# A row gradient on one core: the first store of every three tiles waits for the second tile's vector pass, and Pool places the first tiles' row ends

## The chip, the cores and the metric

The kernel runs on one core of a Trainium2 chip. The metric is the device time of one execution in microseconds (us); before the change it is 1247.63 us, the median of three runs (1247.45 to 1247.71). The core has a vector engine (DVE), a general engine (POOL), a scalar engine (ACT) and a matrix engine (PE), of which the last two do nothing here, and a sync engine (SP), which issues all transfers. The transfers run on 16 DMA engines.

## The reference

`x` is an 8192 x 8192 array of float32, and the result is its gradient along the rows:

```python
def reference(x):
    return np.gradient(x, axis=1)
```

For an inner column `j` that is `(x[:, j+1] - x[:, j-1]) / 2`; for the first column it is `x[:, 1] - x[:, 0]`, for the last one `x[:, -1] - x[:, -2]`.

## The kernel before

The rows are cut into 32 tiles ("sets"). A tile holds 256 rows: each of the 128 partitions has `R` = 2 whole rows side by side, 2 x 8192 floats or 64 KB, so that a tile is 8.39 MB and one load or one store moves it in one piece. Three buffers, `slots[0]` to `slots[2]`, take the tiles in turn (`NB` = 3, tile `i` in slot `i % 3`). A slot is `SH` = 64 floats longer than a tile: a load fills it from position 64 on, and the result is written from position 0 on, so that the result overwrites the input in place, a little behind the reading.

For each tile the following is done, in the order of the program:

1. The load (line 60), issued by SP.
2. POOL's subtraction (line 70) computes the four row-end differences of each partition (two rows, two ends) and keeps them in the small buffer `ends`. It waits for the load.
3. DVE's pass (line 76) computes half the difference of the neighbours over the whole slot, 16382 elements per partition, in one instruction. It waits for step 2. The values at the row ends come out wrong there, since the pass runs over the seam between the two rows.
4. The placement (line 87) copies the four values from `ends` over the row ends. It waits for step 3 and runs on POOL for the tiles with `i % 5` equal to 1 or 3 (except for the last two tiles), else on DVE.
5. The store (line 89), issued by SP when the placement is done.

The order of the work is written out by hand (`manual_schedule`), and what waits for what is given by the helper `chain`, which keeps only the waits named in its arguments. SP works through its list in order, and so an instruction that waits holds up those behind it. The list is: loads 0, 1, 2; stores 0, 1, 2; loads 3, 4, 5; stores 3, 4, 5; and so on, with the loads of the next group of three behind the third store of the group before (line 91). Load `i` waits until store `i - 3` has landed, because it fills the same slot. The last group has two tiles only, 30 and 31.

Of the kernel before, what the change touches and what calls it, by code (L numbers as in the profile page):

```python
# [1 line left out]

# [4 lines left out]


@with_exitstack
def kernel(  # L10
    ctx: ExitStack,
    tc: tile.TileContext,
    x: bass.AP,
    out: bass.AP,
):

    nc = tc.nc
    P = nc.NUM_PARTITIONS
    n, m = x.shape
    R = 2
    NB = 3  # L30
    SH = 64
    W = R * m
    nsets = n // (P * R)
    f32 = x.dtype

    x_sets = x.rearrange("(s p t) m -> s p (t m)", p=P, t=R)
    out_sets = out.rearrange("(s p t) m -> s p (t m)", p=P, t=R)

    pool = ctx.enter_context(tc.tile_pool(name="pool", bufs=1))
    slots = [pool.tile([P, SH + W], f32, name=f"slot{k}", tag=f"slot{k}") for k in range(NB)]  # L40
    ends = pool.tile([P, nsets, R, 2], f32, name="ends", tag="ends")
    loads, stores = [], [None] * nsets
    in_front = {}

    def chain(i, ins, *needed):

        group, engine = f"slot{i % NB}", ins.ins.engine
        keep = [o.ins for o in needed]  # L50
        if in_front.get(engine, (None,))[0] == group:
            keep.append(in_front[engine][1])
        tc.declare_no_dep(ins.ins, group=group, keep=keep, reason="implied by the needed step")
        tc.add_to_no_dep_group(group, ins.ins)
        in_front[engine] = group, ins.ins
        return ins

    def load(i):
        b = slots[i % NB]
        ins = nc.sync.dma_start(out=b[:, SH : SH + W], in_=x_sets[i])  # L60
        loads.append(chain(i, ins, *([stores[i - NB]] if i >= NB else [])))

    with tc.manual_schedule():
        for i in range(NB):
            load(i)
        for i in range(nsets):
            b = slots[i % NB]
            xin = b[:, SH : SH + W].rearrange("p (t m) -> p t m", m=m)

            ins = nc.gpsimd.tensor_sub(  # L70
                out=ends[:, i, :, :],
                in0=xin[:, :, 1 : m : m - 2],
                in1=xin[:, :, 0 : m - 1 : m - 2],
            )
            at = [chain(i, ins, loads[i])]
            ins = nc.vector._custom_dve(  # L76
                dve_ops.TENSOR_TENSOR_REDUCE_SUB_MAX,
                out=b[:, 1 : W - 1],
                in0=b[:, SH + 2 : SH + W],
                in1=b[:, SH : SH + W - 2],  # L80
                s0=0.0,
                s1=0.5,
            )
            halved = chain(i, ins, *at)
            res = b[:, 0:W].rearrange("p (t m) -> p t m", m=m)
            placer = nc.gpsimd if i % 5 in (1, 3) and i < nsets - 2 else nc.vector
            ins = placer.tensor_copy(out=res[:, :, 0 : m : m - 1], in_=ends[:, i, :, :])  # L87
            placed = chain(i, ins, halved)
            ins = nc.sync.dma_start(out=out_sets[i], in_=b[:, 0:W])
            stores[i] = chain(i, ins, placed)  # L90
            if i % NB == NB - 1:
                for k in range(i + 1, min(i + 1 + NB, nsets)):
                    load(k)


# [1 line left out]
_INS = ['x']  # L97
_OUTS = [((8192, 8192), 'float32')]


# [23 lines left out]
```

## Time and profile before

| | |
|---|---|
| Median of three runs | 1247.63 us |
| The profiled execution | 1247.59 us, of which the span from the first to the last instruction is 1245.7 us |
| DVE's pass (line 76) | 32 times, 17224 ns each, 551.2 us in all |
| POOL's row-end differences (line 70) | 32 times, 198 ns each |
| Placements (line 87) | DVE 20 times, 172 ns each; POOL 12 times, 190 ns each |
| Moved by the DMA engines | 536.88 MB, half read and half written, 431 GB/s over the span |
| From issue to landing | load 58.0 us, store 40.4 us (medians); the shortest store 20.9 us |

The times of a row in the timeline are its start and its duration, counted from the start of the span; an "x1" is one instruction, and in brackets stands how long the engine had been idle before it, and what ended that. "SPq" is the issuing of transfers by SP; such a row tells when the transfer was handed over, not how long it took. From issue to landing a transfer also waits behind those that are queued before it.

### The profile page before, as it was taken

The numbers are of one execution on the slowest core, as the hardware profiler recorded it, in microseconds if no ns is written. First come the engines' busy times: TensorE is split into PE (matmuls) and PEld (weight loads), VectorE is DVE, ScalarE is ACT, GpSimd is POOL, SyncE is SP. The second block draws the span as 40 slices with busy tenths as digits, with TensorE's granted clock in tenths as the row PEclk, the third lists the DMA queues.
The fourth block names the chain that finished last, engine by engine and source line by source line (L and its number), as shares of the span: only waits on it lengthen the run. The fifth ranks groups of instructions, "written<-read, shape, count | busy, mean of one in ns | idle before, by whom it ended". The sixth has DMA issues, their size and how long they took to land.

```text
span 1245.7 us, 237 instructions
## 1 busy us (share of the span) xinstructions
DVE 554.6 (45%) x52; POOL 8.8 (1%) x48
## 2 busy tenths in 40 slices
DVE  2850583069009702850582079009603840591083
POOL 0000000000000000000000000000000000000000
DMA  9999999999999999999999999999999999999999
GB/s 404 438 436 423 427 431 438 438 438 436 436 427 431 425 438 436 425 434 436 429 434 436 434 436 434 436 434 438 419 436 436 434 438 438 431 434 429 429 410 404
DMA packets 9217, 536.88 MB, mean 431 GB/s; under 512 B 1024, under 2 KB 1024, under 8 KB 1024
## 3 DMA queue, kind: packets, MB, share of 16 engines
q1 hardware_dynamic: 9216, 536.88, 99.8%
q14 instruction: 1, 0.01, 0.0%
HBM read 268.44 MB, written 268.44 MB: 431 GB/s over the span
## 4 chain that ended last, share of the span: by engine, by line
another core or an unknown queue 74%; DVE 18%; DMA 3%; issue 2%; POOL 1%; SPq 0%; POOLq 0%
DVE slot L76 18%; DMA slot<-in_x_dram 3%; POOL ends L70 0%; POOL slot L87 0%; SPq L60 0%; POOLq L119 0%; DVE slot L87 0%
## 5 line engine op out<-in xcount | busy, mean ns | idle before, releaser
L76 DVE CUSTOM_DVE_ANT_0 slot<-slot 128x16382 f32<-128x16382 f32 x32 | 551.2, 17224 | 668.7 <-POOL ends L70 668.7
L70 POOL TENSOR_TENSOR ends<-slot 128x4 f32<-128x4 f32 x32 | 6.3, 198 | 989.6 <-DMA slot<-in_x_dram 989.6
L87 POOL COPY slot<-ends 128x4 f32<-128x4 f32 x12 | 2.3, 190 | 207.9 <-DVE slot L76 207.9
L87 DVE COPY slot<-ends 128x4 f32<-128x4 f32 x20 | 3.4, 172 | 0.7
L108 POOL MEMSET const-bfloat16-1.0<- 128x1 bf16 x1 | 0.1, 101 | 0.0
L108 POOL MEMSET const-uint8-127<- 128x1 uint8 x1 | 0.1, 101 | 0.0
L108 POOL MEMSET const-float32-0.0<- 128x1 f32 x1 | 0.1, 98 | 0.2 <-issue 0.2
L108 POOL MEMSET const-float32-1.0<- 128x1 f32 x1 | 0.1, 98 | 0.0
## 6 DMA issues: line engine op xcount, KB each, us to landing
slot<-in_x_dram SPq DMA_DIRECT2D x32, 58.0
out_dram<-slot SPq DMA_DIRECT2D x32, 40.4
```

The source lines that it names most:

```text
L70: ins = nc.gpsimd.tensor_sub(out=ends[:, i, :, :], in0=xin[:, :, 1 : m : m - 2], in1=xin[:, :, 0 : m - 1 : m - 2],)
L76: ins = nc.vector._custom_dve(dve_ops.TENSOR_TENSOR_REDUCE_SUB_MAX, out=b[:, 1 : W - 1], in0=b[:, SH + 2 : SH + W], in1=b[:, SH : SH + W - 2],
L87: ins = placer.tensor_copy(out=res[:, :, 0 : m : m - 1], in_=ends[:, i, :, :])
L108: nc = _bacc.Bacc("TRN2", target_bir_lowering=False, num_devices=1)
```

## The change

The placement of the first tile of each group of three (`i % NB == 0`) goes to POOL, and all the other ones to DVE. The store of such a first tile is moved in the program behind the second tile's pass, and gets a wait for that pass besides the one for its own placement. The last group of two tiles is left as it was: its stores wait only for their own placements, which are on DVE. The order of SP's list is the same as before.

```diff
+    def store(i, placed):
+        ins = nc.sync.dma_start(out=out_sets[i], in_=slots[i % NB][:, 0:W])
+        stores[i] = chain(i, ins, placed)
+        return ins
+
+    def store_behind(i, placed, other):
+        tc.add_manual_dep(
+            store(i, placed).ins,
+            other.ins.name,
+            mybir.DependencyInfo(mybir.DependencyClass.Sync, mybir.DependencyReason.DATA),
+            reason="the first store of a group goes behind the second tile's difference",
+        )
+
...
+            opens = i % NB == 1 and i < nsets - 2
...
-            halved = chain(i, ins, *at)
+            halved = chain(i, ins, halved)
+            if opens:
+                store_behind(i - 1, placed, halved)
             res = b[:, 0:W].rearrange("p (t m) -> p t m", m=m)
-            placer = nc.gpsimd if i % 5 in (1, 3) and i < nsets - 2 else nc.vector
+            placer = nc.gpsimd if i % NB == 0 and i < nsets - 2 else nc.vector
             ins = placer.tensor_copy(out=res[:, :, 0 : m : m - 1], in_=ends[:, i, :, :])
             placed = chain(i, ins, halved)
-            ins = nc.sync.dma_start(out=out_sets[i], in_=b[:, 0:W])
-            stores[i] = chain(i, ins, placed)
+            if i % NB or i >= nsets - 2:
+                store(i, placed)
```

More of the change, by code (lines that the diff above doesn't have):

```diff
@@ L4 @@
 import concourse.tile as tile
-from concourse import bass_utils, dve_ops
+from concourse import bass_utils, dve_ops, mybir
 from concourse._compat import with_exitstack
@@ L74 @@
             )
-            at = [chain(i, ins, loads[i])]
+            halved = chain(i, ins, loads[i])
             ins = nc.vector._custom_dve(
```

## The prediction

> **What bounds the kernel now.** I read the page's busy shares and DMA lines first, then the queues, the chain, and the timeline around one change from loads to stores.
>
> ```profile
> DVE 554.6 (45%) x52; POOL 8.8 (1%) x48
> DMA  9999999999999999999999999999999999999999
> ...
> q1 hardware_dynamic: 9216, 536.88, 99.8%
> ```
>
> No compute engine is half busy, while the 16 DMA engines are taken 99.8% of the span, all by one queue, the one SP issues. So the bound is 64 transfers of 8.39 MB (32 loads, 32 stores) one behind the other. A wait on DVE or POOL costs only if it lets this queue run dry. The chain of waits agrees: it gives 74% to "another core or an unknown queue" (its name here for transfers still in flight) and 18% to DVE's pass, which merely lies beside them.
>
> Next, the timeline from the end of tile 3's vector pass to that of tile 5 (second group of three; SPq rows are the issues; POOL L70 starts 0.07 us after a load has landed):
>
> ```profile
> 157.41 0.19 POOL L87 COPY slot<-ends 128x4 f32<-128x4 f32 x1 [17.32 <-DVE slot L76]
> 157.63 0.34 SPq L89 DMA_DIRECT2D out_dram<-slot  x1
> 159.25 0.20 POOL L70 TENSOR_TENSOR ends<-slot 128x4 f32<-128x4 f32 x1 [1.65 <-DMA slot<-in_x_dram]
> 159.48 17.22 DVE L76 CUSTOM_DVE_ANT_0 slot<-slot 128x16382 f32<-128x16382 f32 x1 [2.13 <-POOL ends L70]
> 176.74 0.17 DVE L87 COPY slot<-ends 128x4 f32<-128x4 f32 x1
> 176.94 0.34 SPq L89 DMA_DIRECT2D out_dram<-slot  x1
> 178.70 0.20 POOL L70 TENSOR_TENSOR ends<-slot 128x4 f32<-128x4 f32 x1 [19.25 <-DMA slot<-in_x_dram]
> ```
>
> Store 3 is issued at 157.63, a whole transfer before load 5 lands (178.63), so it waits in the queue behind loads 4 and 5. The next lines are the one place where a store is issued late, store 30 near the end (nothing is loaded behind load 31):
>
> ```profile
> 1186.93 0.20 POOL L70 TENSOR_TENSOR ends<-slot 128x4 f32<-128x4 f32 x1 [77.07 <-DMA slot<-in_x_dram]
> ...
> 1204.62 0.34 SPq L89 DMA_DIRECT2D out_dram<-slot  x1
> 1206.28 0.20 POOL L70 TENSOR_TENSOR ends<-slot 128x4 f32<-128x4 f32 x1 [19.14 <-DMA slot<-in_x_dram]
> ```
>
> Load 31 follows load 30 by 1206.28 - 1186.93 = 19.35 us. That is the undisturbed price of a transfer: eight packets of 64 KB on each DMA engine, 2.418 us each in the DMA records.
>
> **Where the queue loses time today.** Measure each group's third load the same way, by POOL L70's start for the third tile minus that for the second: 20.40 (42.04 to 62.44), 19.45, 19.51, 20.05, 19.85, 19.79, 19.45, 19.84, 19.33, 19.36. Minus 19.35 each, the excess is 1.05 + 0.10 + 0.16 + 0.70 + 0.50 + 0.44 + 0.10 + 0.49 - 0.02 + 0.01 = 3.53 us. The whole stretch from load 1 landed to load 31 landed (42.04 to 1206.28, 60 transfers) is 1164.24 - 60 x 19.35 = 3.24 us too long, so practically all the loss sits in these third loads. The DMA records place it: the last 64 KB packet of the third load, just before a store already queued, takes 2.5 to 3.8 us instead of 2.42, on most engines. At load 31, with no store queued until the last moment, the last packet is not stretched on any engine (excess at most 0.008 us).
>
> **The change, part by part.**
>
> *The late store.* Ten first stores (tiles 0, 3, ..., 27) now wait for the pass over the next tile. For tile 3: the pass over tile 4 ends at 159.48 + 17.22 = 176.70; SP follows a finished engine by 0.03 to 0.06 us in the rows above, so the issue goes from 157.63 to about 176.76, 19.1 us later. Behind it on SP's queue stand stores 4 and 5 and loads 6 to 8. Store 4 must follow the 0.34 us issue: about 177.1 instead of 176.94, not due at the engines until store 3 is through (about 197.9); the rest is issued from 196.39 on. So of the queue's items only store 3 itself can come late.
>
> *Does it come late?* Unstretched, load 5 lands at 159.18 + 19.35 = 178.53, 1.77 us after the new issue. Store 30 was issued 1206.21 - 1204.62 = 1.59 us before load 31 landed, and landed 20.9 us after its issue, at 1225.5: 19.3 us behind load 31, so nothing was lost. The changed stores have 0.18 us more. In the DMA records store 30's first packets start 0.84 to 1.22 us after the issue, which for store 3 is 177.60 to 177.98; the slowest engine is at work on load 5 until about 158.80 + 19.34 = 178.14. That engine sees no gap, by 0.16 to 0.54 us; faster ones do, but the landing waits for the slowest anyway. Bounds of this cost: 0 from store 30; above, the other transfer that started on an idle queue, load 0, landed 21.9 us after its issue, which would make store 3 land at 198.66 instead of 178.53 + 19.35 = 197.88, 0.78 us per group or 7.8 in ten. I take 0, because store 30 is the same kind of transfer in the same place, and load 0 is a cold start (its own first packets took 3 us).
>
> [...]
>
> *The stretched packet.* If the stretch comes from the store queued behind the load, as load 31 suggests, the late store removes it: 3.53 us at most. Bounds: the whole 3.53, or 0 if it is a property of the change from reading to writing; I take the whole, by the row of load 31, though loads 26 and 29 (-0.02 and 0.01) also show none with a store queued, so this row is weak evidence.
>
> *Re-alignment.* Today the 16 engines drift apart: the landings of one transfer spread over 0.6 us at the start, 3.0 at the end. A new store holds back engines more than the above margin ahead of the slowest, so each group starts nearly level, and small stretches on changing engines (first packets of a group's first load: up to 0.15, 0.34, 0.15, 0, 0.23, 0.13, 0.26, 0, 0.27, 0.20 us on the worst engine in the DMA records, 1.73 in all) can each become the slowest's. Bounds 0 and 1.73; I take half, 0.85, since the margin absorbs those on engines that are ahead.
>
> *Placements.* First tiles go to POOL (10 copies of 190 ns by L87's row), all second and third ones to DVE (172 ns). They lie in DVE's and POOL's idle time: after the copy at 157.41, POOL still waited 1.65 us for the next load, DVE 2.13. The store that follows is not due for 19 us. Cost 0; were that cover gone, 10 x 0.19 = 1.9 us. Nothing on DVE, POOL or SP waits newly but the stores.
>
> **Sum.** The profiled execution took 1247.59 us (span 1245.7, 1.9 around it), 0.04 below the median of the runs. 1247.59 - 3.53 + 0.85 + 0 = 1244.9.
>
> **The rivals.**
>
> *The stretch stays* (22%). It belongs to the turn from reads to writes, and the late store changes nothing. For: loads 26 and 29 were not stretched although a store was queued, so the queue alone does not decide. Then each group pays its worst engine: the records' maxima are 1.40, 0.40, 0.31, 0.78, 0.91, 0.53, 0.40, 0.71, 0.07, 0.35, sum 5.86 against 3.53 paid now, at most +2.3; or the same as now if margins absorb that. 1247.6 to 1249.9, mostly 1248.
>
> *Level engines make it worse* (15%, slower). The largest stretch, 1.05, came at the first group, when the engines stood within 0.6 us; at 3 us apart it was about 0. If the stretch grows when all turn at once, re-alignment gives every group the first one's price: 10 x 1.05 - 3.53 = +7.0, 1254.6. It decides from a mean of 0.60 us per group on (3.53 + 2.5 = 6.0 over ten). Against: the second and third groups stood nearly as level (0.8 us) and lost 0.10 and 0.16.
>
> *The queue runs dry* (8%). Load 0's latency holds: +7.8 - 3.53 = +4.3, 1251.9. The store 30 row speaks against it.
>
> **How the numbers follow.** The forecast case (55%) has its own range: 1244.0 (all of the stretch, nothing for re-alignment) to 1246.3 (1.73 for re-alignment and 0.5 left of the stretch). A change of 0.2%, 2.5 us, is about what a measurement of this kernel can tell from none. The case passes that bound in about seven of ten: 38% faster. Within it lie the rest of the case and most of the first rival, 17 + 20 = 37%. Slower: 2 + 15 + 8 = 25%. The range 1243.9 to 1251.0 holds the forecast case, the first rival and a small part of the other two, about 80%.
>
> **What would show it.** SP's first store of a group starts 0.03 to 0.1 us after the second tile's pass, some 1.8 us before the third load lands. Third-load intervals of POOL L70 (now another line) near 19.35 in all groups show the stretch gone; 19.4 to 20.4 as before, the first rival; all near 20.4, the second. The queue has run dry if the next group's first load comes later than 4 x 19.35 = 77.4 us after the third one of this group, or the DMA share falls at the turns. The forecast is wrong if intervals stay as they were or the four-transfer ones grow past 77.5. POOL L87 should show 10 copies, DVE's 22, and no new wait.

## The result, and the profile after

The changed kernel takes 1253.16 us (median of five runs, 1252.26 to 1253.45) against 1247.71 us of the kernel before in the same series: a ratio of 1.004 (95% interval 1.0029 to 1.005). It is slower by 0.4%, where 1244.9 us was forecast.

The profiled execution took 1252.26 us, with a span of 1250.0 us, 4.3 us more than before. From its page, the busy shares, the DMA line and the queue, and from its groups the two forms of placement:

```profile
DVE 554.9 (44%) x54; POOL 8.5 (1%) x46
DMA  9999999999999999999999999999999999999999
...
q1 hardware_dynamic: 9216, 536.88, 99.9%
...
L103 DVE COPY slot<-ends 128x4 f32<-128x4 f32 x22 | 3.8, 172 | 0.8
L103 POOL COPY slot<-ends 128x4 f32<-128x4 f32 x10 | 1.9, 192 | 173.2 <-DVE slot L90 173.2
```

The bytes and packets are the same, and the queue is "busy" all the time as before. That share does not help here: a packet that takes longer also counts as busy. The same stretch of the second group in the timeline after (start and duration in us):

```profile
157.64 0.19 POOL L103 COPY slot<-ends 128x4 f32<-128x4 f32 x1 [17.32 <-DVE slot L90]
159.47 0.20 POOL L84 TENSOR_TENSOR ends<-slot 128x4 f32<-128x4 f32 x1 [1.63 <-DMA slot<-in_x_dram]
159.70 17.22 DVE L90 CUSTOM_DVE_ANT_0 slot<-slot 128x16382 f32<-128x16382 f32 x1 [2.12 <-POOL ends L84]
176.96 0.82 SPq L64 DMA_DIRECT2D out_dram<-slot  x2
176.96 0.17 DVE L103 COPY slot<-ends 128x4 f32<-128x4 f32 x1
178.82 0.20 POOL L84 TENSOR_TENSOR ends<-slot 128x4 f32<-128x4 f32 x1 [19.15 <-DMA slot<-in_x_dram]
```

Store 3 now goes out at 176.96, 0.04 us after the pass over tile 4, and store 4 right behind it (the x2). The third load takes 178.82 - 159.47 = 19.35 us: the 0.10 us of stretch that it had before is gone. The next landing, that of tile 6's load, is where the time went. POOL's rows of line 84 alone, of the second group and the first load of the third:

```profile
159.47 0.20 POOL L84 TENSOR_TENSOR ends<-slot 128x4 f32<-128x4 f32 x1 [1.63 <-DMA slot<-in_x_dram]
178.82 0.20 POOL L84 TENSOR_TENSOR ends<-slot 128x4 f32<-128x4 f32 x1 [19.15 <-DMA slot<-in_x_dram]
256.91 0.20 POOL L84 TENSOR_TENSOR ends<-slot 128x4 f32<-128x4 f32 x1 [77.89 <-DMA slot<-in_x_dram]
```

From 178.82 to 256.91 three stores and a load pass through the queue: 78.09 us, where 4 x 19.35 = 77.40 are due. Before the change the same stretch took 256.24 - 178.70 = 77.54 us:

```profile
178.70 0.20 POOL L70 TENSOR_TENSOR ends<-slot 128x4 f32<-128x4 f32 x1 [19.25 <-DMA slot<-in_x_dram]
256.24 0.20 POOL L70 TENSOR_TENSOR ends<-slot 128x4 f32<-128x4 f32 x1 [77.34 <-DMA slot<-in_x_dram]
```

Two intervals of each group thus hold the whole story: that of the third load (second tile's POOL start to the third's, 19.35 undisturbed) and that of the four transfers behind it (77.40 undisturbed). Summed over ten groups, in us above undisturbed:

| run (profiled execution) | third loads | four transfers behind | sum |
|---|---|---|---|
| before | 3.53 | -0.23 | 3.30 |
| after | -0.04 | 7.70 | 7.66 |

The difference of the sums, 4.36 us, is the difference of the spans. The DMA records say which packet it is: in every group after the change the last 64 KB packet of the third store, the one just before the next group's first load, takes 0.62 to 0.70 us longer in the mean of the 16 engines (2.42 us is normal; the worst engine 0.85 to 1.11). It is as long (0.65 to 0.68) in the three groups in which no engine stood idle for more than 0.04 us ahead of the first store; in the others the longest idle time of an engine was 0.14 to 0.63 us. Before the change no third store had a mean stretch above 0.003 us. So the stretch did not vanish, it moved from the turn loads-to-stores to the turn stores-to-loads, and became twice as dear.

### The profile page after: what moved, and what is told of

It is laid out like the page before. It is cut to its first block, busy times and chain, and to the rows that moved or that the text cites. A ratio compares the mean times of both kernels' runs of the same rounds, so it can differ in the third digit from the quotient of the medians.

```text
span 1250.0 us, 237 instructions
## 1 busy us (share of the span) xinstructions
DVE 554.9 (44%) x54; POOL 8.5 (1%) x46
## 3 DMA queue, kind: packets, MB, share of 16 engines
q1 hardware_dynamic: 9216, 536.88, 99.9%
## 4 chain that ended last, share of the span: by engine, by line
another core or an unknown queue 79%; DVE 14%; DMA 3%; issue 2%; POOL 1%; SPq 0%; POOLq 0%
DVE slot L90 14%; DMA slot<-in_x_dram 3%; POOL ends L84 0%; POOL slot L103 0%; SPq L60 0%; POOLq L135 0%; DVE slot L103 0%
```

## The experiments

The theory formed on this: when a store arrives at a queue that is empty or nearly so, the next turn pays for it. The expectations of the first four runs call this the dry-queue theory. Those of the later runs add a mechanism, the read-ahead theory: a DMA engine that has work queued reads ahead for the next packets while it writes the last ones; a store that arrives when an engine has all but finished the load finds that lead gone, and the next turn pays to get it back. Rivals: the moved placements; the wait as such, or two stores close together; 16 engines that turn all at once ("level engines").

**Placements alone.**

```diff
-            placer = nc.gpsimd if i % 5 in (1, 3) and i < nsets - 2 else nc.vector
+            placer = nc.gpsimd if i % NB == 0 and i < nsets - 2 else nc.vector
```

> Only the placements move (first tiles to POOL, all others to DVE); the first store of a group is issued as before. Dry-queue theory (the queue is empty or nearly so when the late store arrives, and the stretch then comes at the next turn, from stores to loads): no late store, so 1247.7 within 1, third loads stretched by 0 to 1 us, third stores not at all. Placement theory (the moved copies delay something): 1253, third stores stretched by 0.8 us.

Measured: 1248.52 us against 1247.87, ratio 1.0004 (0.9995 to 1.0014); third loads +3.90 us, four transfers -0.32. The placements cost nothing that can be told, as the prediction had it.

**The wait alone** (the changed kernel with the old `placer` line).

> Only the wait of the first store for the second tile's pass; the placements stay with i % 5. Dry-queue theory: 1253 as after the whole change, third loads at 19.35 us, the last packet of every third store longer by about 0.65 us in the mean of the 16 engines. Placement theory: 1247.7, or 1245 if the late store alone brings what was forecast.

Measured: 1252.42 us, ratio 1.0035 (1.0023 to 1.0048); third loads +0.21, four transfers +8.12. The late store alone brings the whole loss.

**The late store in every other group.**

```diff
-            opens = i % NB == 1 and i < nsets - 2
+            opens = i % (2 * NB) == 1 and i < nsets - 2
...
-            if i % NB or i >= nsets - 2:
+            if i % (2 * NB) or i >= nsets - 2:
```

> The late store in every other group only (tiles 0, 6, 12, 18, 24); the first stores of tiles 3, 9, 15, 21, 27 are issued early as before. Dry-queue theory: the third stores of the treated groups alone are stretched by about 0.8 us, those of the others not, and the third loads ahead of tiles 3, 9, ... may be; 1249.5 to 1251. Level-engines theory (what stretches is that all 16 engines turn within half a us, which the treated groups bring about for the others too): third stores of all groups stretched, 1252 to 1253.

Measured: 1255.97 us, ratio 1.0065 (1.005 to 1.008): with half as many late stores the kernel is slower still, which neither theory had foreseen in size. POOL's rows of line 84 from the second group (early store) to the fourth (early again):

```profile
180.12 0.20 POOL L84 TENSOR_TENSOR ends<-slot 128x4 f32<-128x4 f32 x1 [20.55 <-DMA slot<-in_x_dram]
257.47 0.20 POOL L84 TENSOR_TENSOR ends<-slot 128x4 f32<-128x4 f32 x1 [77.15 <-DMA slot<-in_x_dram]
...
276.79 0.20 POOL L84 TENSOR_TENSOR ends<-slot 128x4 f32<-128x4 f32 x1 [1.61 <-DMA slot<-in_x_dram]
296.15 0.20 POOL L84 TENSOR_TENSOR ends<-slot 128x4 f32<-128x4 f32 x1 [19.16 <-DMA slot<-in_x_dram]
374.99 0.20 POOL L84 TENSOR_TENSOR ends<-slot 128x4 f32<-128x4 f32 x1 [78.64 <-DMA slot<-in_x_dram]
...
394.36 0.20 POOL L84 TENSOR_TENSOR ends<-slot 128x4 f32<-128x4 f32 x1 [1.66 <-DMA slot<-in_x_dram]
415.11 0.20 POOL L84 TENSOR_TENSOR ends<-slot 128x4 f32<-128x4 f32 x1 [20.56 <-DMA slot<-in_x_dram]
```

The group with the late store has an undisturbed third load (296.15 - 276.79 = 19.36) and dear transfers behind it (374.99 - 296.15 = 78.84). The group with the early store is the reverse: 77.35 behind it (257.47 - 180.12), but its third load takes 20.75 (415.11 - 394.36), 1.4 us too much. All ten groups alternate in that way; the early ones' third loads take 20.28 to 20.75, as only the first group's did before (20.40). So a late store costs twice: at the next turn from stores to loads, and at the next turn from loads to stores unless that one is made late as well. As a cause of the stretched third stores, level engines are out: the third stores of the first two groups of the kernel before are not stretched (0.00), though the engines stand within 0.6 and 0.8 us of each other there, and neither are those of the early groups here (0.7 to 2.1 us apart). The third loads of the early groups need another look, since 0.9 to 1.4 us each is about what the prediction's rival of that name had forecast (1.05), and the engines are 0.4 to 1.2 us apart ahead of the last packet there, which is longer by 0.76 to 1.11 us in the mean. But level engines alone do not do it: in the second groups of the kernel before and of the run with the placements alone they stood within 0.8 and 0.6 us of each other, also with a store queued, and that packet was longer by 0.19 us only.

**The wait moved to the second tile's load** (POOL's difference instead of DVE's pass).

```diff
             halved = chain(i, ins, loads[i])
+            if opens:
+                store_behind(i - 1, placed, halved)
...
             halved = chain(i, ins, halved)
-            if opens:
-                store_behind(i - 1, placed, halved)
```

> The first store of a group waits for POOL's row-end difference of the second tile, which starts when that tile's load has landed, instead of for its pass: issued near 159.5 us in the second group, 17 us earlier than after the change and 2 us later than before, with the whole third load still ahead of it. Dry-queue theory: the queue never runs dry, 1247.7 within 1, third loads stretched as before, third stores not. If the wait on another tile's step or the order of issue is what costs: 1253.

Measured: 1248.29 us, ratio 1.0002 (0.9993 to 1.0011); third loads +3.37, four transfers -0.64. With the third load still ahead of it the store may wait for another tile's step: not the wait costs, but its end so near to the third load's.

**An eighth of the store early.** The late store is as late as after the change, but the engines have 1 MB of it to go on with.

```diff
+    def store_early(i, placed):
+        ins = nc.sync.dma_start(out=out_sets[i][:, 0:C], in_=slots[i % NB][:, 0:C])
+        early[i] = [chain(i, ins, placed)]
...
             if i % NB or i >= nsets - 2:
                 store(i, placed)
+            else:
+                store_early(i, placed)
```

(`C` = `W // 8`; the late part moves columns `C` to `W`, and the load into that slot waits for both.)

> As after the change, but an eighth of the first store (columns 0 to 2047 of a partition's 16384, 1 MB, 2.4 us) goes out early, as soon as that tile's ends are placed, and only the other seven eighths wait for the second tile's pass. The late store is as late as after the change, but the engines have the eighth to go on with. Read-ahead theory: the turn from loads to stores is made with a fed queue, third stores not stretched, third loads stretched as before, 1247.7 to 1249 (ten DMAs more). If a late issue near the turn costs in itself, or level engines do: 1253.

Measured: 1250.69 us, ratio 1.0022 (1.0012 to 1.0031), above what was expected. The intervals answer the question all the same: four transfers -0.15, so the stretch behind is gone, and third loads +5.57, stretched again, by 2.0 us more than before, which is nearly all of the 2.2 us by which the span (1247.9) exceeds that before. Why they lose more stays open. The seven eighths are issued at 176.95 in the second group, as after the change, with store 4 right behind them; so neither a late issue near the turn nor two stores close together stretches the third store if the engines are fed.

**The other side: loads that start on an empty queue.** The kernel before, with

```diff
+        if i and i % NB == 0:
+            tc.add_manual_dep(
+                ins.ins,
+                stores[i - 1].ins.name,
+                mybir.DependencyInfo(mybir.DependencyClass.Sync, mybir.DependencyReason.DATA),
+                reason="the first load of a group goes behind the third store",
+            )
```

> The kernel before, with the first load of a group (3, 6, ...) waiting for the third store in front of it to land, so that the queue runs empty at the turn from stores to loads instead of that from loads to stores. Read-ahead theory: besides the open gap (1.5 to 2 us per turn, 10 turns) the lead is lost there, and the next turn, loads to stores, pays as the first group of the kernel before does, whose queue also starts empty: every third load at 20.3 to 20.5 us, no third store stretched; 1247.7 + 15 to 20 for the gaps + 7 for the stretches = 1270 to 1275. If the stretches have nothing to do with an empty queue: third loads as before (19.3 to 20.4, by 0.35 us in the mean), 1263 to 1268.

Measured: 1280.38 us, ratio 1.0258 (1.0244 to 1.0272), 5 us above what was expected. POOL's rows (line 77 here) in the second group:

```profile
161.73 0.20 POOL L77 TENSOR_TENSOR ends<-slot 128x4 f32<-128x4 f32 x1 [1.65 <-DMA slot<-in_x_dram]
182.09 0.20 POOL L77 TENSOR_TENSOR ends<-slot 128x4 f32<-128x4 f32 x1 [20.16 <-DMA slot<-in_x_dram]
262.31 0.20 POOL L77 TENSOR_TENSOR ends<-slot 128x4 f32<-128x4 f32 x1 [80.02 <-DMA slot<-in_x_dram]
```

The third load takes 20.36 us, and so it is in every group (20.05 to 20.75): the stretch that the kernel before has fully in its first group alone, whose loads also start on an empty queue. The miss is in the gap: the four transfers take 80.22, 2.8 too long, made of 1.9 us of idle engines and 0.7 us of slow first packets, where 1.5 to 2 in all had been put.

**How late is too late.** The second tile's pass is cut in two on DVE, and the first store waits for the first part only.

```diff
-            ins = nc.vector._custom_dve(
...
+            cuts = [1, W - W // 8, W - 1] if opens else [1, W - 1]
+            for a, z in zip(cuts, cuts[1:]):
+                ins = nc.vector._custom_dve(
...
+                halved = chain(i, ins, halved)
+                if opens and a == 1:
+                    store_behind(i - 1, placed, halved)
```

With `W // 32`, `W // 16` and `W // 8`:

> As after the change, but the second tile's pass is cut in two (31/32 and 1/32) and the first store waits for the first part only, so that it is issued some 0.5 us earlier: its packets are there about 0.8 us before the engines are through with the third load instead of 0.2. Read-ahead theory (a fed DMA engine reads for the next packets while it still writes the last; a store that arrives after the reading is done finds that lead gone, and the next turn, stores to loads, pays 0.65 to 0.8 us to get it back; how far ahead the lead reaches is not known, about 1 to 2 us by the stretches of 0.7 and 1.1): third stores still stretched, by 0.3 to 0.8, 1250 to 1253. If only a queue that really stands empty costs: nothing is empty here, 1247.7 or, with neither stretch, 1244.

> The same with the cut at 15/16, the first store issued about 1.0 us earlier than after the change and there 1.3 us before the third load's end. Read-ahead theory: part of the lead kept, third stores stretched by 0 to 0.5 us, third loads by part of what they were before, 1246 to 1250. Empty-queue theory: 1247.7 or less.

> The same with the cut at 7/8, the first store issued about 2.1 us earlier than after the change and there 2.3 us before the third load's end. Read-ahead theory: lead kept, third stores not stretched, third loads as before the change, 1247.7 within 1. If the wait for a vector pass as such costs, or that the first two stores come close together: 1253.

and, chosen by what these showed, `W // 12` and `W // 10`:

> The late store with the second tile's pass cut at 11/12: issued some 1.4 us earlier than after the change, about 2.8 us before the slowest engine is through with the third load. Read-ahead theory, by the packets of the runs with the cuts at 31/32, 15/16 and 7/8: an engine whose third load ends 2.4 to 3 us after the store's issue pays next to nothing at either turn, one at under 1.4 us pays 0.65 us at the next, one at 4 us 0.5 us at this one. Slowest engine in that window, those ahead of it lose only what they are ahead: 1244.5 to 1247, faster than the kernel before by 1 to 3 us. If the window is chance: between the neighbours, 1248 to 1250.

> The same with the cut at 9/10, issued some 1.7 us earlier than after the change, about 3.1 us before the slowest engine's end. Read-ahead theory: at the upper edge of the window, third loads stretched by 0 to 0.2 us on the slowest engine, 1245 to 1248; between the cuts at 11/12 and 7/8 in time. If the window is chance: 1248 to 1250.

| run | us, all executions | ratio to before | third loads | four transfers |
|---|---|---|---|---|
| after (no cut) | 1252.26 to 1253.45 | 1.004 (1.0029 to 1.005) | -0.04 | 7.70 |
| cut 31/32 | 1249.61 (1248.42 to 1252.05) | 1.0015 (1.0006 to 1.0024) | 0.24 | 7.24 |
| cut 15/16 | 1247.76 (1246.10 to 1251.30) | 0.9999 (0.9988 to 1.001) | 2.83 | 2.57 |
| cut 11/12 | 1250.26 (1245.86 to 1250.76) | 1.0013 (1.0004 to 1.0022) | 3.35 | 1.66 |
| cut 9/10 | 1250.45 (1247.42 to 1251.18) | 1.0015 (1.0006 to 1.0024) | 3.99 | 1.12 |
| cut 7/8 | 1249.84 (1248.75 to 1250.49) | 1.0014 (1.0005 to 1.0023) | 2.94 | 1.27 |

The two intervals are of one profiled execution each (those of the cuts took 1252.05, 1250.51, 1250.29, 1249.98 and 1249.17 us; that of 31/32 was the slowest of its ten, that of 15/16 took 2.8 us more than the median). The cost moves from the one turn to the other as the store comes earlier. The DMA records show the rule behind it engine by engine. The margin is the time from the store's issue to the end of that engine's last packet of the third load; the seven runs with the late store in all groups (after, the wait alone, five cuts) give 1120 cases, the runs with an early store (before, placements alone, wait for the load) 480. The records name no engine; a packet is put to the engine whose packet before it ended as it began:

| margin of the engine | cases | mean stretch, last packet of the third store | mean stretch, last packet of the third load |
|---|---|---|---|
| below 1.4 us | 617 | 0.67 | 0.00 |
| 1.4 to 1.8 | 192 | 0.39 | 0.01 |
| 1.8 to 2.4 | 127 | 0.15 | 0.01 |
| 2.4 to 3.0 | 85 | 0.09 | 0.05 |
| 3.0 to 3.4 | 54 | 0.02 | 0.17 |
| 3.4 to 5 | 45 | 0.01 | 0.39 |
| 16 to 22 (early stores) | 480 | 0.00 | 0.31 |

Between 2.4 and 3.0 us an engine pays almost nothing at either turn. The attempts to hit that window did not beat the kernel before. The margins of the 16 engines lie up to 3.4 us apart in those runs, so that some pay at each turn, and the landing waits for the slowest; that this is why they did not win was not tested by itself. Single executions were faster: one of eleven with the cut at 11/12 took 1245.86, and five of ten with that at 15/16 took 1246.10 to 1246.66, below any of the kernel before in their series (lowest 1247.09 and 1247.01); the other five took 1248.86 to 1251.30. The trace kept is of one of the slow five, so what sets the fast ones apart stays open. Of the forecasts, 1247.7 within 1 for the cut at 7/8 (1249.84) and 1245 to 1248 for that at 9/10 (1250.45) were too low, and 31/32 came just below its 1250 to 1253. The forecast of 1244.5 to 1247 for the cut at 11/12 was wrong too: it reckoned with the slowest engine's margin and took the others' loss as covered by what they were ahead.

## Why the prediction was wrong, point by point

*What bounds the kernel*: right. The queue decides, DVE, POOL and SP do not; the moved placements cost nothing (the run with them alone).

*The late store arrives in time*: right. It was issued 0.2 us later than reckoned (176.96 for 176.76; load 4 had landed that much later) and its first packets started 0.84 to 1.41 us after it in groups two to ten, the row of store 30 having given 0.84 to 1.22. In eight of the ten groups the end of the last engine shows no loss at the first store (0.15 and 0.48 us in the other two). The first store starts without a gap on the slowest engine, and the loss sits at the end of the third store, at the turn to a load that had been queued two transfers ahead (issued at 198.11 in the second group).

*The stretched packet goes away*: right, and wholly: 3.53 us of it before, -0.04 after.

*Re-alignment*: the engines did come level, their spread before the third load's last packets fell from 0.6 to 3.1 us to 0.4 to 0.8. The 0.85 us of cost put on it was not found where it was looked for: the first loads of the groups lost 0.38 us in sum on the slowest engine, 0.40 of that in the first group alone.

*The step that failed* is the sentence that of the queue's items "only store 3 itself can come late", and with it a sum without a term for the turn from stores to loads. That turn had cost nothing in any group before, and I took it as untouched because its own transfers are queued as early as ever. The row of store 30, which carried the argument, could not show it: no load follows store 30. In the runs the term is 0.62 to 1.48 us per group, 7.70 in ten, measured by the four transfers' interval. That interval past 77.5 us was among the prediction's own signs of being wrong, and it came in every group.

*The rivals*: "the queue runs dry" (8%) came out near the time, 1251.9, and near the interval, 78.18 per group against 78.02 to 78.31 in nine of ten. Its mechanism was half right: the queue did hold nothing behind the packets in flight, but the cost is not a late start of the first store. That 7.70 us came out so near its 7.8 is luck. "The stretch stays" and "level engines make it worse" are refuted by the third loads of the changed kernel (19.33 to 19.36), whose engines are level. The early ones of the alternating groups do pay the price that the latter rival had named, but level engines elsewhere do not (0.19 us, above).

What is shown is when the cost falls due: a turn is stretched if the engines' queue stood empty, or within about 2 us of it, at the turn before. The run with an early eighth, the loads on an empty queue and the margins all agree on that. It is not the only case: the early groups of the alternating run pay at the turn to stores though their own loads were queued in good time; there it is the turn before that one that was made late. That the engines' reading ahead is what gets lost is an inference; no record shows the inside of an engine. Why the later groups of the kernel before still lose 0 to 0.7 us with a queue that is never empty stays open too.

## What to carry to other kernels

When one queue bounds a kernel, a wait that ends just in time need not be free, even if no engine stands idle for it: look at the next changes between loads and stores, not only at the transfer that was held back. Measure each turn by the interval between landings on either side of it, since the busy share of the DMA engines (99.8% and 99.9% here) cannot show a packet that takes longer. And an example in the trace that seems to prove a new order harmless must also have the work behind it that the new order will have; store 30 was the last turn of the program.

## What was not expected of the hardware

Starting on an empty queue costs at the next change of direction: 0.62 to 0.70 us in the mean of the engines if it was stores that started (after the change, then at the turn to loads), 0.83 to 1.21 us if it was loads (the run with late loads, at the turn to stores). A turn to stores that was made with a queue fed 16 us or more ahead left the next turn, to loads, free: the third stores of all three runs with early stores, 480 cases, had a mean stretch of 0.00. The other way round it does not hold: the last packets of their third loads were stretched by 0.23 us in the mean of groups two to ten. With one late store in every other group both prices are paid, which made half the change dearer (ratio 1.0065) than the whole (1.004).
